# Two fused transformer layers in fp32: a Silu moved behind the feed-forward's copies, and a step of other matmuls put in front of three groups of transposes

## The chip, the cores and the metric

The kernel runs on one core of a Trainium2 chip. The core's engines are TensorE (PE in the profile, its weight loads PEld), VectorE (DVE), ScalarE (ACT), GpSimd (POOL), and SyncE (SP), which issues the transfers (DMA). Each engine takes its instructions in the order in which the program gives them, and waits at the first whose inputs are not there. The metric is the device time of one execution in microseconds (us), given as the median of several runs; lower is better.

## The reference, cut to what matters

Two layers over 1024 positions of width 1024, all in float32. The first mixes a gated delta rule (4 heads, chunks of 64 in the reference) with stick-breaking attention; the second has two kinds of attention, a feed-forward net with a causal convolution, and a small gate at the end. The change touches the delta rule, the projections in front of it, and the feed-forward net:

```python
# first layer
proj = jnp.einsum('bsd,dp->bsp', xn, w_in)
qkv_a = jax.nn.silu(_causal_dwconv(proj[..., :A_QKV1], conv_w)).astype(f32)
q_a = _l2n(qkv_a[..., :nqk].reshape(b, s, DN_HEADS, DN_DK))
...
decay = jnp.exp(jnp.where(causal, gc[..., :, None] - gc[..., None, :], -jnp.inf))
kk = jnp.einsum('bhnid,bhnjd->bhnij', k, k)
m = jnp.where(strict, beta[..., :, None] * kk * decay, 0.0)
sol = lax.linalg.triangular_solve(eye + m, rhs, left_side=True, lower=True, unit_diagonal=True)
...
# second layer
def conv_ffn(h, w_gate, w_up, conv_w, conv_b, w_down):
    s = h.shape[1]
    g = h @ w_gate
    gp = jnp.pad(g, ((0, 0), (CONV_WIDTH - 1, 0), (0, 0)))
    conv = conv_b
    for j in range(CONV_WIDTH):
        conv = conv + gp[:, j:j + s, :] * conv_w[j]
    return (jax.nn.silu(conv) * (h @ w_up)) @ w_down
```

## The kernel before, in words

**Products.** A float32 product is made as three passes of matmuls: every operand is split into a high part (a rounded cast, on ACT) and a low part (what is left, a subtraction on POOL), and high by high, high by low and low by high are summed in PSUM (lines L260 to L262, and L1531 in the feed-forward). A framework orders each engine's instructions by priorities before the program is built; what that order is, the lists in the section on the change show.

**Projections in front of the delta rule (`proj_a`).** Twelve tiles of 128 channels. For each, `conv` does the causal convolution on VectorE (L510, then three times L512) and a Silu on ScalarE (L514, output `conv_s`); `post` then transposes the tile on TensorE (L526, four at a time), and VectorE scales the result into `conv_kv` (L535), which is stored to DRAM (L536). `post` of a tile is issued one projection later than its `conv`; the last two, tiles 10 and 11, have no projection behind them any more.

**The fill.** `fill` is a list of 84 steps of independent work for the other half of the layer (`proj_b`: a projection through `qk_stack`, 48 matmuls of 128x256 a step at its start, then a normalisation: squares on ACT, L738 and L739 on VectorE, a reciprocal root by twelve small VectorE operations `rs_...` of L287 to L302, and a multiplication on POOL, L746). `mix` interleaves it with a main generator: at each `yield` of that one, steps of the fill are issued until both stand at the same share.

**The delta rule (`gdr`).** Eight chunks of 128 positions in two lanes, even and odd, each chunk in 19 steps with a `yield` between them; the second lane begins nine rounds later. Of a chunk: POOL makes `G` (L591), a matmul sums it (L593), ScalarE takes exponentials; products of keys (L608); VectorE makes `NT`; then, in one step, POOL scales `qk` (L616), VectorE makes `XT` from `NT` in two operations (L618, L619), TensorE transposes it (L622), and ScalarE copies the result. A blocked inversion follows (L633, L640).

**The feed-forward (`ffn`).** Eleven rounds (`gi`) of 256 channels. Each has two products, gate and up, each by a Strassen-Winograd scheme (`wino`) of seven half-size products; one of these (`mul`) is 12 matmuls of 128x512. Order of the muls in a product: B11, B21, T2, T1, T3, T4, B22. B11, T2 and T3 add up in one PSUM tile, `x`; between them `keep` copies the sum so far to SBUF (`u1`, `u2`, `u3`, all L1535 on ACT), and the next mul into `x` waits for that copy. `out(ct, half, ...)` hands a finished quarter to VectorE: of the gate product L1567 into `f_u`, of the up product L1582 and L1583. When the gate product is done, VectorE does the convolution over `f_u` for both channel tiles `ct` (L1573 once and L1575 twice for each) and ScalarE a Silu of each (L1576). ScalarE also does the casts of the weights, one mul's at a time and seven muls ahead (L1511), and POOL the low parts (L1512) and the sums of weights (L1517).

Of the kernel before, what the change touches and what calls it, by code (L numbers as in the profile page):

```python
# [15 lines left out]
AF = mybir.ActivationFunctionType  # L16
# [147 lines left out]
class Kern:  # L164
# [22 lines left out]
    def PT(self, shape=(128, 4, 128)):  # L187

        return self.pt.tile(list(shape), F32, tag="pj" if self.pt is self.pj else "pt", name="pt")
# [193 lines left out]
    def layer1(self):  # L383
        nc, d, tc, vec = self.nc, self.d, self.tc, self.vec
        dr = lambda n, s: self.dram.tile(s, F32, name=n)
        self.dr_x = dr("dr_x", [T, D])
        self.dr_v = dr("dr_v", [2, NT, 128, 256])
        self.dr_gate = dr("dr_gate", [128, 16, 1024])
        self.dr_z = dr("dr_z", [2, 128, 4, 1024])
        self.dr_qk = dr("dr_qk", [4, 128, 4, 1024])  # L390
        self.dr_oa = dr("dr_oa", [2, 128, 4, 1024])
        self.dr_qa = dr("dr_qa", [128, 8, 1024])
        self.dr_kv = dr("dr_kv", [128, 2, 4, NT, 128])
        with self.pool("xn1") as xnp:
            self.xn = [self.pair(xnp, f"xn1_{h}") for h in range(2)]
            zp, zp_close = self.open("zp", 2)
            fill = Fill(chain(self.proj_b(), self.proj_z(zp)), 84)
            with self.pool("gdr0") as self.gp:
                with self.pool("cv", 2, "right") as self.cv, self.banks(4, 4):
                    with self.pool("nrm1", 1, "right") as np_:  # L400
                        get = self.loader(d["x"], np_, nc.sync)
                        get(0)
                        g1 = self.gain(np_, "g_n1")
                        get(1)
                        self.wahead = 0
                        wv = self.W(d["w_vba"])
                        get(2)
                        get(3)
                        w = self.W(d["w_qa"][0])
                        self.wahead = 400  # L410
                        get(4)
                        for f in self.later:
                            f()
                        self.norm_half(get, g1, self.xn[0], np_, 0)
                        self.norm_half(get, g1, self.xn[1], np_, 1)
                    self.proj_a(wv, w)
                with self.pool("pb", 1, "right") as self.pb, self.banks(2, 0):
                    self.mix(self.gdr(), fill, 0.43)
            b = self.banks(2, 1)
            self.mix(self.sb(), fill, 0.9)  # L420
            b.close()
            self.pjs = self.banks(5, 3)
            self.mix(self.merge_in(), fill)
            zp_close()
# [65 lines left out]
        self.nb2 = gp.tile([128, 32], F32, name="nb2")  # L490
        nc.vector.tensor_scalar(self.nb2, self.b2, -1.0, None, ALU.mult)

    def proj_a(self, wv, w):
        nc, d, gp, cv = self.nc, self.d, self.gp, self.cv
        ba = gp.tile([128, NT, 8], F32, name="ba")

# [60 lines left out]
        for c in range(2, 12):  # L557
# [5 lines left out]
            post(*pend.pop(0))  # L563
            pend.append((c, conv(c, u)))
        for p in pend:
            post(*p)

    def gdr(self):
# [13 lines left out]
        def chunk(c):  # L582
# [34 lines left out]
            XT = tl("XT")  # L617
            nc.vector.tensor_tensor(XT, NTt, bc(self.m2t), ALU.mult)  # L618
            nc.vector.tensor_tensor(XT, XT, bc(self.ident), ALU.add)  # L619
            px = PT()  # L620
            for h in range(4):
                nc.tensor.transpose(px[:, h, :], XT[:, h, :], self.ident)  # L622
# [87 lines left out]
        n, done = 0, 0  # L710
        while lanes[0] or lanes[1]:
            for p in range(2):
                if p == 1 and n < 9:
                    continue
                if lanes[p]:
                    if next(lanes[p][0], 1) == 1:
                        lanes[p].pop(0)
                        if lanes[p]:
                            next(lanes[p][0])
                    done += 1  # L720
                    yield min(1.0, done / 150)
            n += 1
        es.close()

# [769 lines left out]
        np_close()  # L1494
        m1_close()

    def wino(self, src, pool, out, ahead=400):


        nc = self.nc  # L1500
# [32 lines left out]
        def keep(ps, n):  # L1533
            v = pool.tile([128, 512], F32, tag=f"w_{n}", name=f"w_{n}", bufs=2)
            nc.scalar.copy(v, ps)  # L1535
            return v
        x, z, y = self.PJ(), self.PJ(), self.PJ()
        mul(x, w1, "B11")
        u1 = keep(x, "u1")
        mul(z, w2, "B21")  # L1540
        out(0, 0, z, u1)
        mul(x, w6, "T2", False)
        u2 = keep(x, "u2")
        mul(y, w5, "T1")
        mul(x, w7, "T3", False)
        u3 = keep(x, "u3")
# [7 lines left out]
    def ffn(self):  # L1554

        nc, d, tc, vec = self.nc, self.d, self.tc, self.vec
        with self.pool("ffn", 1) as fp:
            for gi in range(11):
                us, ys = [], []
                for _ in range(2):  # L1560
                    u = fp.tile([128, 2 + T], F32, tag="f_u", name="f_u", bufs=2)
                    nc.vector.memset(u[:, 0:2], 0.0)
# [4 lines left out]
                    nc.vector.tensor_tensor(u, ps, v, ALU.add)  # L1567
                self.wino(d["w_fg"][gi], fp, gate)
                cw = vec["cw2"]
                for ct in range(2):  # L1570
                    c, u = 2 * gi + ct, us[ct]
                    y = fp.tile([128, T], F32, tag="f_y", name="f_y", bufs=2)
                    nc.vector.tensor_scalar(y, u[:, 0:T], cw[:, c, 0:1], vec["cb2"][:, c:c + 1], ALU.mult, ALU.add)  # L1573
                    for j in range(1, 3):
                        nc.vector.scalar_tensor_tensor(y, u[:, j:j + T], cw[:, c, j:j + 1], y, ALU.mult, ALU.add)  # L1575
                    nc.scalar.activation(y, y, AF.Silu)  # L1576
                    ys.append(y)

                def up(ct, half, ps, v):
                    y = ys[ct][:, half * 512:half * 512 + 512]  # L1580
                    c = fp.tile([128, 512], F32, tag="f_c", name="f_c", bufs=1)
                    nc.vector.tensor_tensor(c, ps, v, ALU.add)  # L1582
                    nc.vector.tensor_tensor(y, y, c, ALU.mult)  # L1583
                self.wino(d["w_fu"][gi], fp, up, 400 if gi else 100)
                for ct in range(2):
                    nc.sync.dma_start(self.dr_h[2 * gi + ct], ys[ct])
        self.xb_close()
# [93 lines left out]
```

## Time and profile before

| What | us |
|---|---|
| runs of the kernel before | 2677.5, 2668.34, 2666.72 |
| median of them | 2668.34 |
| the profiled execution, its own time | 2666.2 |
| its span in the profile | 2664.3 |
| TensorE busy in it | 2486.0 (93%) |
| VectorE, GpSimd, ScalarE busy | 1467.1, 1060.1, 856.4 |

The profiled execution took 2666.2 us; the span from the first to the last instruction is 1.9 us less. Sums of the trace are made against that execution, whose time lies 2.1 us under the median of the runs. The mean TensorE clock granted was 0.98 of full speed. TensorE is the engine that is busy nearly always, so that time is to be had almost only where it waits; the busy times of the others say little by themselves.

### The profile page before, as it was taken

To read this page: it belongs to the slowest core of one execution; us is meant where nothing else is said; L and a number is where in the kernel's file an instruction comes from. 1 tells how busy PE (TensorE), PEld (TensorE's weight loads), DVE (VectorE), ACT (ScalarE), POOL (GpSimd) and SP (SyncE) were. 2 spreads that over 40 slices of the span, in tenths; PEclk is the share of its full clock that TensorE was granted. 3 is DMA by queue.
4 is the path that set the end of the run, shared out by engine and by line. 5 is a ranking of instruction groups with operands and counts; after the bars stand their busy time and mean duration, and the time that the engine had idled before them with its cause. 6 is when DMAs were issued, how large, how long until landed. Compare 5 with 4: busy or idle time off the path is not lost.

```text
span 2664.3 us, 38694 instructions
## 1 busy us (share of the span) xinstructions
PE 2486.0 (93%) x15170; PEld 2114.7 (79%) x15170; DVE 1467.1 (55%) x2837; ACT 856.4 (32%) x1559; POOL 1060.1 (40%) x922
## 2 busy tenths in 40 slices
PE   6998999999999999999889969899999999999999
PEld 6888888976777778989777748888777777777789
DVE  6565555366666554457844537657445435534372
ACT  3322222254444342122324425554333333200030
POOL 2524322121222244544533222322787777533322
PEclk9999999999999999999999989999999999999999
DMA  4423222253422355322674356562222222523222
GB/s 162 145 103 109 82 84 77 67 154 103 124 83 72 134 191 183 106 85 80 200 218 140 111 168 180 165 208 88 63 82 77 80 79 68 201 79 111 72 84 92
DMA packets 153006, 313.54 MB, mean 118 GB/s; under 512 B 14164, under 2 KB 57428, under 8 KB 152696
## 3 DMA queue, kind: packets, MB, share of 16 engines
q1 hardware_dynamic: 152824, 311.07, 37.5%
q8 instruction: 120, 1.97, 0.3%
q14 instruction: 62, 0.51, 0.1%
HBM read 214.01 MB, written 100.42 MB: 118 GB/s over the span
## 4 chain that ended last, share of the span: by engine, by line
PE 54%; DVE 13%; DMA 5%; ACT 4%; issue 4%; POOL 1%; SPq 0%; ACTq 0%; DVEq 0%; POOLq 0%
PE pj L1531 15%; PE pj L262 9%; PE pj L261 9%; PE pj L260 9%; PE po L916 3%; PE pt L912 2%; DVE cs L876 2%; DVE e L873 1%; DMA m_o<-dr_oa 1%; PE po L1339 1%; DVE aT L914 1%; DVE cs L877 1%; DMA dr_dqk<-qb_st 1%; DMA dr_mla<-l_st 1%; DVE rs_a L300 1%
## 5 line engine op out<-in xcount | busy, mean ns | idle before, releaser
L251 POOL TENSOR_SCALAR hl<-raw 128x512 fp32r<-128x512 f32 (+3 forms) x270 | 196.4, 733 | 932.7 <-PE pj L262 920.0
L252 POOL TENSOR_TENSOR hl<-raw,hl 128x512 fp32r<-128x512 f32 (+3 forms) x270 | 372.3, 1385 | 16.1
L260 PE MATMUL pj<-hl,xn_0h 128*128 128x256 f32 (+2 forms) x544 | 161.2, 297 | 2.0 <-DVE qb_st L310 1.2
L261 PE MATMUL pj<-hl,xn_0h 128*128 128x256 f32 (+2 forms) x544 | 160.9, 296 | 1.7 <-POOL hl L252 1.7
L262 PE MATMUL pj<-hl,xn_0l 128*128 128x256 f32 (+2 forms) x544 | 160.0, 294 | 0.0
L260 PE MATMUL pj<-hl,xn_1h 128*128 128x256 f32 (+2 forms) x544 | 158.4, 291 | 0.0
L262 PE MATMUL pj<-hl,xn_1l 128*128 128x256 f32 (+2 forms) x544 | 158.0, 290 | 0.0
L261 PE MATMUL pj<-hl,xn_1h 128*128 128x256 f32 (+2 forms) x544 | 157.5, 289 | 0.0
L1512 POOL TENSOR_TENSOR hl<-w_s,hl 128x512 fp32r<-128x512 f32 x88 | 121.8, 1384 | 83.2 <-ACT hl L1511 82.9
L262 PE MATMUL pj<-hl,f_hl 128*128 128x512 f32 x352 | 140.5, 401 | 2.8 <-DVE f_hl L1613 2.7
L260 PE MATMUL pj<-hl,f_hh 128*128 128x512 f32 x352 | 140.0, 398 | 2.6 <-DVE xres L1622 2.1
L261 PE MATMUL pj<-hl,f_hh 128*128 128x512 f32 x352 | 138.2, 393 | 0.0
L914 DVE COPY aT<-pt 128x512 f32<-128x512 f32 (+1 forms) x128 | 80.5, 629 | 102.6 <-PE pt L912 101.7
L1622 DVE TENSOR_TENSOR xres<-xres,pj 128x512 f32<-128x512 f32 x96 | 65.2, 686 | 126.4 <-PE pj L262 114.6
L1512 POOL TENSOR_TENSOR hl<-raw,hl 128x512 fp32r<-128x512 f32 x66 | 99.2, 1508 | 71.4 <-ACT hl L1511 70.8
L1567 DVE TENSOR_TENSOR f_u<-pj,w_u 128x512 f32<-128x512 f32 x44 | 30.5, 692 | 170.3 <-ACT w_u L1535 96.4
L916 PE MATMUL po<-aT,v 128*64 128x128 f32 x1152 | 98.2, 287 | 26.1 <-DVE aT L914 21.1
L916 PEld LDWEIGHTS po<-aT,v 128*64 128x64 f32 x1152 | 59.8, 136 | 73.2 <-DVE aT L914 53.3
L260 PE MATMUL pj<-xn_0h,hl 128*128 128x512 f32 x288 | 116.9, 406 | 0.0
L260 PE MATMUL pj<-xn_1h,hl 128*128 128x512 f32 x288 | 115.8, 402 | 0.0
L262 PE MATMUL pj<-xn_1h,hl 128*128 128x512 f32 x288 | 115.5, 401 | 0.0
L262 PE MATMUL pj<-xn_0h,hl 128*128 128x512 f32 x288 | 115.1, 400 | 0.0
(594 smaller groups left out, 7392.9 us busy)
## 6 DMA issues: line engine op xcount, KB each, us to landing
raw<-in_w_o_dram SPq DMA_DIRECT2D x28, 512.0 KB
qk<-dr_mla SPq DMA_DIRECT2D x32, 416.0 KB
dr_mla<-l_st SPq DMA_DIRECT2D x32, 384.0 KB
raw<-in_w_fg_dram SPq DMA_DIRECT2D x22, 512.0 KB
raw<-in_w_fu_dram SPq DMA_DIRECT2D x22, 512.0 KB
dr_h<-f_y SPq DMA_DIRECT2D x22, 512.0 KB
raw<-in_w_fd_dram SPq DMA_DIRECT2D x22, 512.0 KB
f_y<-dr_h SPq DMA_DIRECT2D x22, 512.0 KB
```

The lines of the kernel that those rows point to most:

```text
L251: nc.gpsimd.tensor_scalar(hl[:, 0], raw[:, k:k + c], 1.0, 1.0, ALU.mult, ALU.mult)
L252: nc.gpsimd.tensor_tensor(hl[:, 1], raw[:, k:k + c], hl[:, 0].bitcast(F32), ALU.subtract)
L260: mm(ps, lh[0], rh[0], start=first, stop=False)
L261: mm(ps, lh[0], rh[1], start=False, stop=False)
L262: mm(ps, lh[1], rh[0], start=False, stop=last)
L876: nc.vector.tensor_tensor_scan(cs[:, a, ::-1], self.ones[:, 0:1].to_broadcast([128, nk]), e[:, a, ::-1], 0.0, ALU.mult, ALU.add)
L912: nc.tensor.transpose(pt[:, b, :], e[a][:, j * 128:j * 128 + 128], self.ident)
L914: copy[j0 > 0](aT[:, :n], pt[:, :n])
L916: nc.tensor.matmul(po[64 * a:64 * a + 64, :], v[:, j, a * 64:a * 64 + 64], aT[:, b, :], start=j == 0, stop=j == i)
L1512: nc.gpsimd.tensor_tensor(hl[:, 1], v, hl[:, 0].bitcast(F32), ALU.subtract)
L1531: nc.tensor.matmul(ps, w[k][l], b[r][:, k, :], start=first and k + n == 0, stop=k == 3 and n == 2, skip_group_check=not first)
L1622: nc.vector.tensor_tensor(xr, xr, ps, ALU.add)
```

## The change

Three parts. **(1)** `proj_a` takes `fill`, and does one step of it in front of each of the last two `post`; the pool `pb`, from which these steps draw their tiles, is opened earlier for that, on the other side of SBUF. **(2)** `chunk` has one more `yield`, between `XT` and its transposes, the second lane begins one round later, and the share is counted over 158 instead of 150. **(3)** `keep` can be given something to do behind a copy. In `ffn` the Silu of channel tile 1 is now issued behind the copy `u1` of the up product, that of tile 0 behind the copy `u2`; the convolutions are written for tile 1 first; and quarter (0, 0) of each product is handed out behind `u2`'s copy instead of in front of the mul T2.

```diff
-                    self.proj_a(wv, w)
-                with self.pool("pb", 1, "right") as self.pb, self.banks(2, 0):
+                    self.pb, pb_close = self.open("pb")
+                    self.proj_a(wv, w, fill)
+                with self.banks(2, 0):
                     self.mix(self.gdr(), fill, 0.43)
+                pb_close()
...
         for p in pend:
+            fill.step()
             post(*p)
...
             nc.vector.tensor_tensor(XT, XT, bc(self.ident), ALU.add)
+            yield
             px = PT()
...
-                if p == 1 and n < 9:
+                if p == 1 and n < 10:
...
-                    yield min(1.0, done / 150)
+                    yield min(1.0, done / 158)
...
             nc.scalar.copy(v, ps)
+            if n in then:
+                then[n]()
             return v
...
-        out(0, 0, z, u1)
         mul(x, w6, "T2", False)
         u2 = keep(x, "u2")
+        out(0, 0, z, u1)
...
-                for ct in range(2):
+                ys = {}
+                for ct in (1, 0):
...
-                    nc.scalar.activation(y, y, AF.Silu)
-                    ys.append(y)
+                    ys[ct] = y
+                silu = lambda y: nc.scalar.activation(y, y, AF.Silu)
...
-                self.wino(d["w_fu"][gi], fp, up, 400 if gi else 100)
+                self.wino(d["w_fu"][gi], fp, up, 400 if gi else 100,
+                          {"u1": lambda: silu(ys[1]), "u2": lambda: silu(ys[0])})
```

The lines of the changed kernel stand 3 (delta rule), 4 (`qk_stack` and the later steps of the delta rule) or 5 to 8 (feed-forward) below those of the kernel before: L591 becomes L594, L622 becomes L626, L746 becomes L750, L1535 becomes L1540, L1576 becomes L1585.

**In the feed-forward**, ScalarE's queue around an up product stands so before (L1511 casts weights, L1535 are the copies of `keep`, L1576 the Silu; here 18619 is the convolved tile 0 and 18624 tile 1):

```order
L1511 CAST hl_18778<-raw_18774 128x512
L1511 CAST hl_18781<-raw_18776 128x512
L1535 COPY w_u1_18677<-pj_18662 128x512
L1511 CAST hl_18788<-w_s_18786 128x512
L1576 ACTIVATE f_y_18619<-f_y_18619 128x1024
L1576 ACTIVATE f_y_18624<-f_y_18624 128x1024
L1511 CAST hl_18791<-w_s_18784 128x512
L1535 COPY w_u2_18706<-pj_18662 128x512
```

and so in the changed kernel (18619 is now tile 1, 18623 tile 0):

```order
L1516 CAST hl_18778<-raw_18774 128x512
L1585 ACTIVATE f_y_18619<-f_y_18619 128x1024
L1516 CAST hl_18781<-raw_18776 128x512
L1540 COPY w_u1_18675<-pj_18660 128x512
L1585 ACTIVATE f_y_18623<-f_y_18623 128x1024
L1516 CAST hl_18788<-w_s_18786 128x512
L1516 CAST hl_18791<-w_s_18784 128x512
L1540 COPY w_u2_18702<-pj_18660 128x512
```

The two Silu operations have parted, and the first of them stands in front of a cast and of the copy `u1`, the second between that copy and `u2`: the scheduler has put each ahead of where it is written.

VectorE's queue at the same place, from the last quarters of the gate product (L1567) over the convolution (L1573, L1575) to the first quarter of the up product (L1582), before:

```order
L1567 TENSOR_TENSOR f_u_18772<-pj_18878,w_u3_18875 128x512
L1567 TENSOR_TENSOR f_u_18770<-pj_18809,w_u2_18849 128x512
L1573 TENSOR_SCALAR f_y_18905<-f_u_18770,cw2_75,cb2_76 128x1024
L1573 TENSOR_SCALAR f_y_18910<-f_u_18772,cw2_75,cb2_76 128x1024
L1575 SCALAR_TENSOR_TENSOR f_y_18905<-f_u_18770,cw2_75,f_y_18905 128x1024
L1575 SCALAR_TENSOR_TENSOR f_y_18910<-f_u_18772,cw2_75,f_y_18910 128x1024
```

and in the changed kernel:

```order
L1574 TENSOR_TENSOR f_u_18772<-pj_18878,w_u3_18875 128x512
L1581 TENSOR_SCALAR f_y_18905<-f_u_18772,cw2_75,cb2_76 128x1024
L1583 SCALAR_TENSOR_TENSOR f_y_18905<-f_u_18772,cw2_75,f_y_18905 128x1024
L1574 TENSOR_TENSOR f_u_18770<-pj_18809,w_u2_18848 128x512
L1583 SCALAR_TENSOR_TENSOR f_y_18905<-f_u_18772,cw2_75,f_y_18905 128x1024
L1581 TENSOR_SCALAR f_y_18909<-f_u_18770,cw2_75,cb2_76 128x1024
L1569 MEMSET f_u_19056 128x2
L1583 SCALAR_TENSOR_TENSOR f_y_18909<-f_u_18770,cw2_75,f_y_18909 128x1024 x2
```

The convolution of tile 1 (`f_u_18772`) now begins one quarter of the gate product earlier and is done as a whole ahead of that of tile 0; before, both began behind the last quarter and took turns.

**In front of the delta rule**, GpSimd's queue, from the low parts of a weight (L252) to the first chunk's second operation, before:

```order
L252 TENSOR_TENSOR hl_2400<-raw_2395,hl_2400 128x512
L591 TENSOR_TENSOR G_1843<-cst_85,g_a_826 128x512
L616 TENSOR_TENSOR qk_1839<-qk_1839,EG_1847 128x1024
L591 TENSOR_TENSOR G_2144<-cst_85,g_a_826 128x512
L746 TENSOR_TENSOR qb_raw_1871<-qb_raw_1871,rs_y_2064 128x1024
```

and in the changed kernel:

```order
L252 TENSOR_TENSOR hl_2321<-raw_2316,hl_2321 128x512
L750 TENSOR_TENSOR qb_raw_1806<-qb_raw_1806,rs_y_1982 128x1024
L594 TENSOR_TENSOR G_1967<-cst_85,g_a_829 128x512
L619 TENSOR_TENSOR qk_1963<-qk_1963,EG_1971 128x1024
L594 TENSOR_TENSOR G_2223<-cst_85,g_a_829 128x512
```

The fill's multiplication, which waits for the reciprocal root of that step on VectorE, has moved from behind the first two `G` to in front of them.

**In the delta rule**, TensorE's queue between a chunk's products of keys and its transposes, in a chunk in the middle, before (rows of the fill, L260 to L262, left out at the line of dots):

```order
L608 MATMUL inv<-qk 128x256 x4
L633 MATMUL inv<-X,NT 128x64 x4
L262 MATMUL pj<-hl,xn_0l 128x256
...
L622 MATMUL inv<-cst,XT 128x128 x4
L640 MATMUL inv<-Y,XT 128x64 x4
```

and in the changed kernel:

```order
L611 MATMUL inv<-qk 128x256 x4
L637 MATMUL inv<-X,NT 128x64 x4
...
L644 MATMUL inv<-Y,XT 128x64 x4
L262 MATMUL pj<-hl,xn_0l 128x256
...
L648 MATMUL inv<-cst,X 128x128 x4
L261 MATMUL pj<-hl,xn_0h 128x256
L626 MATMUL inv<-cst,XT 128x128 x4
L654 MATMUL inv<-X,NT 64x64 x4
```

The transposes of `XT` now stand behind one step of the other lane (L644, L648), with fill around it.

## Rows read from the trace of the kernel before

**Rows 1.** Windows: us, busy PE, PEld, DVE, ACT, POOL (instructions); clock, DMA share, GB/s.
```profile
215.00:220.00 5.00, 5.00 (x32) 5.00 (x33) 2.67 (x4) 1.74 (x2) 0.00 (x0) 0.71 0.38 124
...
230.00:520.00 290.00, 273.43 (x2225) 258.07 (x2225) 151.96 (x414) 74.94 (x150) 84.77 (x68) 0.99 0.24 75
```

**Rows 2.** Waits of TensorE, whole span: total us, times, longest.
```profile
PE pj L1531 <- ACT w_u L1535: 13.6, 11, 1.5
...
PE inv L622 <- DVE XT L619: 9.2, 7, 1.9
...
PE pt L526 <- ACT conv_s L514: 4.9, 2, 4.7
```

**Rows 3.** Timeline of TensorE in one round: T2, T1, T3 of the up product.
```profile
1923.62 0.40 PE L1531 MATMUL pj<-T2h,hl 128*128 128x512 f32 x1
...
1926.40 0.40 PE L1531 MATMUL pj<-T1h,hl 128*128 128x512 f32 x1
...
1930.60 0.50 PE L1531 MATMUL pj<-T3h,hl 128*128 128x512 f32 x1 [1.25 <-ACT w_u L1535]
```

**Rows 4.** Timeline of ScalarE in the same round.
```profile
1921.09 0.62 ACT L1511 CAST hl<-raw 128x512 fp32r<-128x512 f32 x1 [2.17 <-PE pj L1531]
1921.62 0.58 ACT L1535 COPY w_u<-pj 128x512 f32<-128x512 f32 x1
...
1927.30 2.26 ACT L1576 ACTIVATE f_y<-f_y 128x1024 f32<-128x1024 f32 x2 [2.77 <-DVE f_y L1575]
```

**Rows 5.** Timeline of VectorE in the same round, cut into single instructions.
```profile
1915.49 0.69 DVE L1567 TENSOR_TENSOR f_u<-pj,w_u 128x512 f32<-128x512 f32 x1 [0.89 <-PE pj L1531]
...
1918.99 1.86 DVE L1573 TENSOR_SCALAR f_y<-f_u,cw,cb 128x1024 f32<-128x1024 f32 x1
...
1920.78 0.80 DVE L1573 TENSOR_SCALAR f_y<-f_u,cw,cb 128x1024 f32<-128x1024 f32 x1
1921.50 1.27 DVE L1575 SCALAR_TENSOR_TENSOR f_y<-f_u,cw,f_y 128x1024 f32<-128x1024 f32 x1
```

**Rows 6.** Timeline of GpSimd in the same round.
```profile
1916.26 1.29 POOL L1512 TENSOR_TENSOR hl<-w_s,hl 128x512 fp32r<-128x512 f32 x1 [0.40 <-ACT hl L1511]
...
1919.00 1.30 POOL L1512 TENSOR_TENSOR hl<-raw,hl 128x512 fp32r<-128x512 f32 x1
```

**Rows 7.** Timelines elsewhere: VectorE, then GpSimd, at two close starts.
```profile
1646.61 1.90 DVE L1324 SCALAR_TENSOR_TENSOR e<-e,a_r 128x512 f32<-128x512 f32 x1
...
2302.04 1.23 DVE L1613 TENSOR_TENSOR f_hl<-f_y,f_hh 128x1024 fp32r<-128x1024 f32 x1 [0.45 <-ACT f_hh L1612]
...
1646.65 1.31 POOL L252 TENSOR_TENSOR hl<-raw,hl 128x512 fp32r<-128x512 f32 x1
...
2302.16 2.27 POOL L252 TENSOR_TENSOR hl<-raw,hl 128x512 fp32r<-128x512 f32 x1
```

**Rows 8.** Timelines in front of the delta rule: VectorE, ScalarE, GpSimd.
```profile
211.79 0.69 DVE L535 TENSOR_TENSOR conv_kv<-pt,srk 128x512 f32<-128x512 f32 x1 [3.59 <-DMA dr_kv<-conv_kv]
212.40 1.28 DVE L512 SCALAR_TENSOR_TENSOR conv_y<-conv_u,cw,conv_y 128x1024 f32<-128x1024 f32 x1
...
225.19 0.17 DVE L297 TENSOR_SCALAR rs_i<-rs_m 128x16 int32<-128x16 int32 x1
...
213.79 1.06 ACT L514 ACTIVATE conv_s<-conv_y 128x1024 f32<-128x1024 f32 x1 [11.44 <-DVE conv_y L512]
...
232.35 1.90 POOL L746 TENSOR_TENSOR qb_raw<-qb_raw,rs_y 128x1024 f32<-128x1024 f32 x1 [2.05 <-DVE rs_y L302]
```

**Rows 9.** Timelines at a chunk's `XT`: VectorE, GpSimd, TensorE.
```profile
402.81 1.78 DVE L618 TENSOR_TENSOR XT<-NT,cst 128x512 f32<-128x512 f32 x1
404.62 1.41 DVE L619 TENSOR_TENSOR XT<-XT,cst 128x512 f32<-128x512 f32 x1
...
401.65 2.39 POOL L616 TENSOR_TENSOR qk<-qk,EG 128x1024 f32<-128x1024 f32 x1 [3.02 <-ACT XT L645]
...
406.18 0.63 PE L622 MATMUL inv<-cst,XT 128*128 128x128 f32 x4 [1.17 <-DVE XT L619]
```

More of the change, by code (lines that the diff above doesn't have):

```diff
@@ L491, in kstats, with proj_a @@
         nc.vector.tensor_scalar(self.nb2, self.b2, -1.0, None, ALU.mult)
-    def proj_a(self, wv, w):
+    def proj_a(self, wv, w, fill):
         nc, d, gp, cv = self.nc, self.d, self.gp, self.cv
@@ L1495, in out2b, with wino @@
         m1_close()
-    def wino(self, src, pool, out, ahead=400):
+    def wino(self, src, pool, out, ahead=400, then={}):
         nc = self.nc
@@ L1558, in ffn @@
             for gi in range(11):
-                us, ys = [], []
+                us = []
                 for _ in range(2):
```

## The prediction

> **What bounds the kernel now.** I read the waits of TensorE first, because that engine is busy 93% of the span: a change can only give time where it stands still, or take time by making it stand. Three of its waits belong to what is changed [rows 2]: the mul T3 waits for a copy in each of the eleven rounds of the feed-forward, 13.6 us in all; the transposes of `XT` wait seven times, 9.2 us; and the last transposes of `proj_a` wait once for 4.7 us. Then I read timelines around one case of each. In the windows the stretch of the delta rule has TensorE busy for 273.43 of 290 us [rows 1]: much more than these waits is not there.
>
> **The feed-forward before.** In the round shown T2 starts at 1923.62 and T1 at 1926.40, so a mul takes 2.78 us and T3 could start at 1929.18. It starts at 1930.60 [rows 3], 1.42 late, and 11 times that is 15.6 us (the waits view models where a matmul ends and gives 13.6). It waits for the copy `u2`, which stands behind both Silu operations, begun at 1927.30 [rows 4], and these wait for the end of the convolution. The convolution is slow because VectorE and GpSimd shut each other out. A TENSOR_SCALAR takes 0.80 alone, but 1.86 when it starts at 1918.99 beside GpSimd's operation at 1919.00; it ends 0.55 behind that one's end at 1920.30 [rows 5, 6]. The other way round, GpSimd's operation of 2302.16 lasts 2.27 instead of 1.3 and ends 1.16 behind VectorE's of 2302.04 to 2303.27 [rows 7]. Each waits for the whole of the other.
>
> **The feed-forward after.** Nothing is added or removed; two Silu operations and half of a convolution move. The convolution of tile 1 can start when L1567 of its last quarter is done, at 1915.49 + 0.69 = 1916.18, some 1916.22 with the 0.04 that lie between two such operations. GpSimd's low part starts at 1916.26 [rows 5, 6]. Which of the two goes first is the question on which this part hangs, since VectorE would be ahead by only about 0.04. In the round of before VectorE was ahead by 0.01 and lost; at 1646.61 it was ahead by 0.04 and lost (1.90 us for 512 columns, and it ended 0.55 behind GpSimd's); at 2302.04 it was ahead by 0.12 and won [rows 5, 6, 7]. The nearest case is a loss, and I take it.
>
> Then: low part to 1917.55; TENSOR_SCALAR to 1918.10; GpSimd's next operation, already waiting, to 1919.26 (+1.16); the first L1575 to 1920.35 (its own time is 1.27 [rows 5]; behind a wait I take 1.1, since part of it is done by then); GpSimd to 1921.5; the second L1575 to 1922.6. The Silu of tile 1 takes 1.06 for that size [rows 8] (1.13 by the pair in [rows 4]), to 1923.7. Behind it in ScalarE's order stand a cast and then `u1`, which are 0.53 apart, and the copy takes 0.58 [rows 4], overlapping a little: done at 1924.7. T2 needs that copy. It started at 1923.62 and will start at about 1924.77: **a new stall of 1.15**, because the first Silu stands in front of `u1`. What is queued behind the Silu is the cast, whose low part is wanted only seven muls later, so that alone costs nothing. The convolution of tile 0 follows: TENSOR_SCALAR to 1923.4, L1575 to 1924.7, one GpSimd operation to 1925.9, L1575 to 1927.0, Silu to 1928.1, two casts, `u2` done near 1929.7. T3 can then start at 1924.77 + 2 x 2.78 = 1930.33, so its own stall is gone, with 0.6 to spare. Saved: 15.6 - 11 x 1.15 = **3.0 us**. The bounds of the term: 15.6 if no stall is left, and below, nothing (a T2 stall as long as the T3 stall was). Handing out (0, 0) behind `u2` moves L1582 of VectorE, for which no matmul waits before the mul B22, eight us later.
>
> The Trainium skill, page "SBUF — State Buffer", section "SBUF: two separate sides", says that VectorE and GpSimd share a port pair as an exclusive lock, and that whichever starts first holds it for its whole instruction. That both shut each other out whole agrees with 1.86 and 2.27; that the first to start wins does not agree with 1918.99 and 1646.61, where the later one by record won. By its rule VectorE would win at 1916.22; that is the first rival below.
>
> **The front.** Before, TensorE has nothing left at 210 and waits 4.7 us for the Silu of tile 11 [rows 2], which ends at 213.79 + 1.06. That Silu waited for L512 of 212.40, and this stood in VectorE's queue behind L535, which waited 3.59 for the store that held its buffer [rows 8]. Then the clock falls: 0.71 was granted from 215 to 220, which is 0.29 x 5 = 1.45 us more. In the changed order all three L512 of tile 11 come ahead of the waiting L535, so the Silu is ready near 210.2. A further 39 matmuls of the fill stand in front of the last transposes: each of the two steps has 48, of which the scheduler had 57 there already. At 273.43 / 2225 = 0.123 us each [rows 1] they take 4.8 us, and fill the gap; as they are taken from later, TensorE's work is the same. Gain: 4.7 + 1.45 = 6.15.
>
> But `G` of the first chunk now stands on GpSimd behind the fill's multiplication L746, and the first matmul of the delta rule needs `G`. From the end of the last transposes: four VectorE operations of 0.69 (two L535, L738, L739), 2.8; twelve small ones of 0.17 and a gap between [rows 8], 2.5; L746, 1.90 [rows 8]; `G`, as 1.3 like other GpSimd operations of 512 columns [rows 6]. Together 8.5, against 4.8 of matmuls that stand in front: a **new wait of 3.7**. TensorE standing that long, I count the clock's 1.45 again. Before, `G` was made long ahead and none of this was there. Net: 6.15 - 5.15 = **1.0 us**. Bounds: +6.15 if the chain is hidden, and -3.8 if none of those matmuls covers it (8.5 + 1.45 - 6.15).
>
> **The delta rule.** The wait at the transposes is one for VectorE: `XT` takes 1.78 and 1.41, since L618 and L619 both lie beside GpSimd's L616, which shuts them out from 401.65 on, and its follower [rows 9]. From the end of L608 near 401.3 to 406.18 this takes 4.9 us. I summed TensorE's work between the two in both orders: 2.9 to 4.4 us before, and 3.9, 4.1, 4.3, 4.3, 5.0, 5.2, 5.6, 7.9 for the eight chunks after, since a step of the other lane and its fill now lie between. Against the 4.9 that leaves 0.9 + 0.8 + 0.6 + 0.6 = 2.9 of waits; of 9.2 some **6.3 us** are saved, bounds 0 (the wait goes on to L633 or L640, the next to need `X`) and 9.2. The lanes keep their pace otherwise: the same fill is spread over 158 shares instead of 150, less the 39 matmuls.
>
> **The sum.** 3.0 + 1.0 + 6.3 = 10.3 us off the profiled execution's 2666.2: **2656 us**. The median of the runs shown is 2668.34, 2.1 above that execution; 2656 is 0.46% under the median. A difference of 0.5%, 13.3 us, is about what a measurement of this kernel can tell from no change: faster means below 2655.0, slower above 2681.7.
>
> **Rivals.**
> *VectorE wins at 1916.22.* Then TENSOR_SCALAR ends at 1917.02, GpSimd at 1918.2, L1575 at 1919.3, GpSimd at 1920.4, L1575 at 1921.5, the Silu at 1922.6, `u1` at 1923.6: T2 stalls 0.04 and T3, by the same steps, 0.14. Saved 15.6 - 2.0 = 13.6 instead of 3.0: 2666.2 - 13.6 - 7.3 = 2645.3. For it: VectorE is ahead, and wins at 0.12; against it: two losses at 0.01 and 0.04. It decides at a lead somewhere between 0.04 and 0.12. The rule of the Trainium skill named above gives this outcome.
> *The delta rule gives nothing.* The chain from `NT` over `XT` and `X` to L633 and L640 is as long as before, and if the other lane's step needs the same VectorE, the wait only goes on to the next matmul. For it: VectorE's 1.78 and 1.41 do not shrink. Against: 2.9 of 9.2 is what the order leaves. 2666.2 - 3.0 - 1.0 = 2662.2, up to 2666 if the front gives nothing too.
> *Slower: the added step lengthens the chain.* Each lane has eight steps more. A step is 290 / 150 = 1.93 us long; if the lanes and not TensorE set the pace, the stretch grows by 8 x 1.93 = 15.5 us. 2666.2 + 15.5 - 3.0 - 1.0 = 2677.7. It ends slower than before once more than 4.0 of these 15.5 us are not covered. For it: at `XT` the lane does set the pace. Against: TensorE is busy 94% of the stretch [rows 1], and the fill is handed out by shares, so it does not run out earlier.
>
> **Chances.** The forecast (GpSimd wins, the front and the delta rule as summed) 0.48, its own range 2649 to 2662; VectorE wins 0.18, 2643 to 2653 by what the delta rule gives; the delta rule gives nothing 0.27; slower than before 0.07. The range that leaves out 2 in 10 goes from 2643 to 2666. Of the forecast a little under half lies below 2655.0, with the first rival 0.41 faster; of the last rival's share about 0.05 lies above 2681.7, since more than one step may be exposed; the rest, 0.54, is within 0.5%.
>
> **What would show it.** In the waits of TensorE after: L1531 for `u2` gone, and a wait of T2 for `u1` of about 1.1, eleven times; if that is 0.1 or less, VectorE won. The TENSOR_SCALAR of tile 1 at 1.8 to 1.9 us says GpSimd won, 0.8 that it lost. The 4.7 us of L526 gone, and a wait of 3 to 4 us at L596 (before L593) for GpSimd's `G`, with a clock near 0.7 behind it. L626 (before L622) waiting for some 3 us instead of 9.2. The prediction is wrong if a wait appears at L637 or L644 as large as the one that goes, if the stretch of the delta rule grows, or if the convolution of tile 0 loses a further turn and `u2` is late as well: each such turn is 1.1 x 11 = 12 us.

## The result, and the profile after

| | us |
|---|---|
| the changed kernel, median of 4 runs | 2649.93 (2642.67 to 2655.23) |
| the kernel before, beside it, 4 runs | 2670.65 (2666.72 to 2677.5) |
| ratio | 0.9915, 95% interval 0.9896 to 0.9933 |
| the changed kernel once more, 5 runs, and before, 14 runs | 2648.8 and 2673.58; ratio 0.9906, 0.989 to 0.9922 |
| span of the profiled execution, before and after | 2664.3 and 2647.3 |

The change makes the kernel faster by 0.9%, which is twice what was forecast: 2656 us had been said, 10.3 us under the profiled execution of before. Between the two traces lie 17.0 us, between the medians 20.7 and 24.8. The execution profiled before was one of the quicker ones of its kernel, so a sum made against it understates what the medians show.

These are the waits of TensorE in the changed kernel over its whole span (total us, times, longest), those that answer to [rows 2] and two new ones:

```profile
PE pj L1536 <- ACT w_u L1540: 10.6, 10, 2.0
...
PE inv L596 <- POOL G L594: 3.0, 1, 3.0
...
PE inv L626 <- DVE XT L622: 1.7, 3, 0.8
...
PE pj L1536 <- DVE f_c L1590: 1.4, 1, 1.4
```

The wait of 13.6 us for `w_u` has become one of 10.6, and a wait for `f_c` has come. The wait for `XT` has gone from 9.2 to 1.7 us. The 4.7 us in front of the last transposes are gone, and 3.0 us for `G` stand there instead. The windows of both kernels show how much time TensorE gained where the delta rule and what stands ahead of it are computed. Columns as in [rows 1]; first the kernel before, a row that answers for the whole stretch:

```profile
190.00:520.00 330.00, 307.82 (x2445) 289.12 (x2443) 174.52 (x445) 82.62 (x163) 99.52 (x78) 0.98 0.26 82
```

and the changed kernel, with three windows of 5 us out of it:

```profile
190.00:520.00 330.00, 319.44 (x2539) 299.78 (x2538) 168.57 (x469) 84.68 (x167) 101.05 (x81) 0.99 0.28 86
215.00:220.00 5.00, 5.00 (x46) 5.00 (x45) 3.35 (x7) 1.88 (x2) 0.00 (x0) 1.00 0.28 105
225.00:230.00 5.00, 4.54 (x24) 3.74 (x25) 0.60 (x1) 2.23 (x6) 0.40 (x1) 1.00 1.03 252
440.00:445.00 5.00, 4.66 (x32) 4.46 (x32) 2.11 (x4) 1.17 (x2) 1.90 (x1) 0.71 0.74 262
```

In 330 us TensorE stands still for 10.6 instead of 22.2 us. The low clock of 215 to 220 is not there, and none came behind the wait for `G`, which ends at 225.5; one is left at 440. So 11.6 of the 17.0 us between the traces are standing time in this stretch.

The round of the feed-forward that answers to [rows 3 to 6], in the changed kernel: TensorE, ScalarE, VectorE and GpSimd.

```profile
1909.96 0.50 PE L1536 MATMUL pj<-T2h,hl 128*128 128x512 f32 x1 [0.95 <-ACT w_u L1540]
...
1907.86 1.07 ACT L1585 ACTIVATE f_y<-f_y 128x1024 f32<-128x1024 f32 x1 [3.71 <-DVE f_y L1583]
1908.83 0.60 ACT L1516 CAST hl<-raw 128x512 fp32r<-128x512 f32 x1
1909.33 0.58 ACT L1540 COPY w_u<-pj 128x512 f32<-128x512 f32 x1
...
1900.71 0.69 DVE L1574 TENSOR_TENSOR f_u<-pj,w_u 128x512 f32<-128x512 f32 x1 [0.89 <-PE pj L1536]
1901.43 1.89 DVE L1581 TENSOR_SCALAR f_y<-f_u,cw,cb 128x1024 f32<-128x1024 f32 x1
1903.36 2.20 DVE L1583 SCALAR_TENSOR_TENSOR f_y<-f_u,cw,f_y 128x1024 f32<-128x1024 f32 x1
...
1901.48 1.29 POOL L1517 TENSOR_TENSOR hl<-w_s,hl 128x512 fp32r<-128x512 f32 x1 [0.40 <-ACT hl L1516]
```

TENSOR_SCALAR starts by record at 1901.43, 0.05 ahead of GpSimd's start, and takes 1.89 (0.80 alone, [rows 5]): GpSimd won, as in the forecast. The Silu then ends at 1908.93, the cast and the copy follow, and T2 starts at 1909.96 behind a wait. T2 waits in ten of the eleven rounds, T3 in none.

### The profile page after: what moved, and what is told of

Same layout as the page of the kernel before. It is cut to its first block, busy times and chain, and to the rows that moved or that the text cites. A ratio compares the mean times of both kernels' runs of the same rounds, so it can differ in the third digit from the quotient of the medians.

```text
span 2647.3 us, 38679 instructions
## 1 busy us (share of the span) xinstructions
PE 2480.8 (94%) x15170; PEld 2111.9 (80%) x15170; DVE 1450.7 (55%) x2837; ACT 855.3 (32%) x1559; POOL 1061.1 (40%) x922
## 4 chain that ended last, share of the span: by engine, by line
PE 50%; DVE 15%; DMA 5%; ACT 4%; issue 4%; POOL 2%; SPq 0%; ACTq 0%; DVEq 0%; POOLq 0%
PE pj L1536 12%; PE pj L262 9%; PE pj L260 9%; PE pj L261 9%; PE po L920 3%; PE pt L916 2%; DVE cs L880 2%; DVE f_y L1583 1%; DVE e L877 1%; DMA m_o<-dr_oa 1%; PE po L1343 1%; DMA f_y<-dr_h 1%; DVE aT L918 1%; DVE cs L881 1%; POOL hl L252 1%
## 5 line engine op out<-in xcount | busy, mean ns | idle before, releaser
L252 POOL TENSOR_TENSOR hl<-raw,hl 128x512 fp32r<-128x512 f32 (+3 forms) x270 | 368.6, 1371 | 16.3
L260 PE MATMUL pj<-hl,xn_0h 128*128 128x256 f32 (+2 forms) x544 | 161.3, 297 | 1.7 <-DVE qb_raw L742 1.1
L262 PE MATMUL pj<-hl,xn_0l 128*128 128x256 f32 (+2 forms) x544 | 160.7, 295 | 0.0
L260 PE MATMUL pj<-hl,xn_1h 128*128 128x256 f32 (+2 forms) x544 | 158.2, 291 | 0.0
L262 PE MATMUL pj<-hl,xn_1l 128*128 128x256 f32 (+2 forms) x544 | 157.0, 289 | 0.0
L262 PE MATMUL pj<-hl,f_hl 128*128 128x512 f32 x352 | 139.8, 399 | 3.7 <-DVE f_hl L1622 3.7
L260 PE MATMUL pj<-hl,f_hh 128*128 128x512 f32 x352 | 139.3, 396 | 3.7 <-POOL hl L252 1.9
L260 PE MATMUL pj<-xn_0h,hl 128*128 128x512 f32 x288 | 117.2, 407 | 0.0
L260 PE MATMUL pj<-xn_1h,hl 128*128 128x512 f32 x288 | 115.8, 402 | 0.0
L262 PE MATMUL pj<-xn_1h,hl 128*128 128x512 f32 x288 | 115.4, 401 | 0.0
L262 PE MATMUL pj<-xn_0h,hl 128*128 128x512 f32 x288 | 115.2, 400 | 0.0
L261 PE MATMUL pj<-xn_0l,hl 128*128 128x512 f32 x288 | 114.6, 398 | 0.0
```

Source lines behind the costliest of these rows:

```text
L252: nc.gpsimd.tensor_tensor(hl[:, 1], raw[:, k:k + c], hl[:, 0].bitcast(F32), ALU.subtract)
L260: mm(ps, lh[0], rh[0], start=first, stop=False)
L261: mm(ps, lh[0], rh[1], start=False, stop=False)
L262: mm(ps, lh[1], rh[0], start=False, stop=last)
```

## The experiments

All ratios are to the kernel before, run beside the others on the same chip. The runs were made in three groups, in which its medians were 2674.39 (the three parts and the pinned order), 2673.58 (the changed kernel once more, the steps behind, the early `G`, the lead) and 2670.25 (one step, three steps, the best). The us given behind a ratio are what its distance from 1 makes of that median.

**The three parts alone.** Each of the three first kernels has one part of the diff and nothing else. The feed-forward:

```diff
+            if n in then:
+                then[n]()
...
+                self.wino(d["w_fu"][gi], fp, up, 400 if gi else 100,
+                          {"u1": lambda: silu(ys[1]), "u2": lambda: silu(ys[0])})
```

> The feed-forward part of the change alone (the Silu operations, the order of the convolutions, quarter (0, 0) later). My theory, by the trace of the changed kernel: the wait of T3 is exchanged for one of T2 that is nearly as long, so this part is worth 1 to 3 us: 0.999 of the time before, T2 late by about 1.1 us in nine rounds, T3 in none. The rival, that the feed-forward gave more than the trace shows because the whole kernel gained 20 us in the median: 0.997 or less.

Measured: 2669.94, ratio 0.9987 (0.9971 to 1.0003). The waits of the feed-forward are those of the changed kernel, and from its first matmul to its last it takes 445.60 us, as in the changed kernel (445.67; before 447.28). Its trace has a use beyond that: from 190 to 520 it is the kernel before, in another execution.

```profile
190.00:520.00 330.00, 308.31 (x2404) 289.82 (x2403) 174.29 (x445) 81.18 (x160) 94.09 (x73) 0.96 0.26 82
210.00:220.00 10.00, 5.42 (x31) 5.22 (x30) 4.55 (x6) 2.94 (x3) 0.00 (x0) 0.66 0.51 187
230.00:240.00 10.00, 8.08 (x44) 7.71 (x43) 4.60 (x14) 1.19 (x2) 3.51 (x3) 0.68 0.19 54
390.00:400.00 10.00, 6.97 (x37) 6.62 (x36) 8.42 (x25) 1.66 (x3) 2.98 (x2) 0.70 0.87 255
```

TensorE is busy as long as before (308.31 against 307.82), but has done 41 matmuls fewer in it, some 7 of them because it came to this stretch 0.9 us later. The three windows of 10 us hold waits of 4.6, 1.9 and 3.0 us and a fall of the clock to the lower of its two levels (1.2 instead of 2.4 GHz); their means are 0.66, 0.68 and 0.70. In the trace of before the same windows have the same waits and 0.83 each: the clock fell there too, for a shorter time.

The yield:

```diff
             nc.vector.tensor_tensor(XT, XT, bc(self.ident), ALU.add)
+            yield
             px = PT()
...
```

> The added step of the delta rule alone (the yield between XT and its transposes, the second lane a round later, 158 shares). Theory 1: the added step hides the wait at the transposes of XT and nothing else: 8 to 9 us, 0.9968, the wait of TensorE for XT falls from 9.2 to about 2 us, and the 4.7 us in front stay. Theory 2: the step also moves the fill against the chunks' other steps, and with that the waits behind the normalisation's transposes (3.0 us for a reciprocal root, 1.2 us more) go too: 11 to 14 us, 0.995. If it is under 3 us, the gain came from the fill's two steps.

Measured: 2667.55, ratio 0.9979 (0.9963 to 0.9994), 5.6 us. The waits of TensorE from 190 to 520 (total us, times, longest):

```profile
PE pt L526 <- ACT conv_s L514: 4.9, 1, 4.9
PE inv L641 <- DVE o_m L697: 3.5, 2, 3.0
PE inv L623 <- DVE XT L619: 3.2, 2, 1.9
```

The wait for `XT` fell from 9.2 to 3.2, nearly as summed. The wait of 3.0 at the inversion stays at the same matmul, now put down to another operation of VectorE, so theory 2 is not what the yield does. Theory 1 is right for the wait and too high for the time: its 8 to 9 us lie at the far end of the interval (1.6 to 9.9), and TensorE's standing time from 190 to 520 falls only from 22.2 to 18.6, since waits of 0.6 to 1.6 us came at other places.

The two steps of the fill:

```diff
         for p in pend:
+            fill.step()
             post(*p)
```

> The two steps of the fill in front of the last transposes alone. Theory: the wait of 4.7 us and the low clock behind it go (6.2 us), a wait of 3 us for the first G comes: 3 us net, 0.9988, and the waits at XT stay at 9 us. Rival: taking 39 matmuls of cover away from the delta rule costs as much there as it gives in front: no difference.

Measured: 2657.79, ratio 0.9944 (0.9927 to 0.996), 15 us. Both expectations failed: by its median this is the largest part of the change, and it had been given 1.0 us in the prediction.

```profile
PE inv L625 <- DVE XT L622: 7.1, 8, 1.2
PE inv L596 <- POOL G L594: 2.9, 1, 2.9
...
PE inv L643 <- DVE rs_a L300: 0.9, 2, 0.6
```

The front is as forecast, a wait of 2.9 for one of 4.7, with a granted clock of 0.74 behind it (225 to 230). The wait for `XT` is shorter too, although nothing was put in front of it, and the 3.0 us at the inversion are gone.

**Where the 15 us come from.** The same two steps, but behind both of the last transposes:

```diff
         for p in pend:
             post(*p)
+        for _ in range(2):
+            fill.step()
```

> The kernel before with the pool opened earlier and the two steps of the fill issued at the same point, but behind both of the last transposes instead of one in front of each: the fill is as far ahead as in the run of that part alone, the gap for the Silu stays (4.7 us), and G does not stand behind the fill's multiplication. Theory 1: most of the 15 us of that part come from where the advance puts the fill's later steps against the chunks (the 3.0 us wait at the inversion goes, and with it a fall of the clock): 8 to 13 us, 0.996. Theory 2: they come from the cover of the gap: within 3 us of before.

Measured: 2664.98, ratio 0.9974 (0.9962 to 0.9986), 7 us (4 to 10). The gap is there, so these 7 us have nothing to do with its cover: theory 1's mechanism, a little under its range.

```profile
PE inv L626 <- DVE XT L623: 7.3, 8, 1.2
PE pt L528 <- ACT conv_s L516: 4.6, 1, 4.6
...
PE inv L644 <- DVE rs_a L300: 0.9, 2, 0.6
```

Behind the front the waits are those of the run with the steps in front: the 3.0 us are gone here too. It is the fill's advance that does this, not its place in front of the transposes. Then one step, and three:

```diff
-        for p in pend:
-            post(*p)
+        post(*pend[0])
+        fill.step()
+        post(*pend[1])
```

> The kernel before with one step of the fill, not two, in front of the last transposes (behind those of tile 10). Theory 1: what the two steps gave beyond the gap is a matter of where the fill's normalisations meet the chunks' steps, so one step gives something else: the 3.0 us wait at the inversion may stay or return elsewhere, and the gain lies anywhere between 2 and 15 us without being half of 15. Theory 2: the advance acts by its length as cover: half of it, 7 us, 0.9973, with half of the change in the waits.

Measured: 2676.77, ratio 1.0017 (1.0001 to 1.0033): no gain, if anything a loss, where both theories had a gain of 2 us or more. The waits of TensorE from 190 to 540, and below them the first of two new ones on TensorE, VectorE and GpSimd:

```profile
PE pt L528 <- ACT conv_s L516: 5.7, 1, 5.7
PE pj L260 <- DVE qb_st L310: 4.8, 1, 4.8
PE st L705 <- POOL ot L701: 3.9, 3, 3.4
...
261.09 0.55 PE L260 MATMUL pj<-hl,xn_0h 128*128 128x256 f32 x1 [4.81 <-DVE qb_st L310]
...
255.44 2.29 DVE L302 SCALAR_TENSOR_TENSOR rs_y<-rs_a,rs_y 128x16 f32<-128x16 f32 x1
...
255.35 2.34 POOL L619 TENSOR_TENSOR qk<-qk,EG 128x1024 f32<-128x1024 f32 x1 [0.19 <-issue]
```

An operation of the fill's normalisation, 0.17 alone, takes 2.29 because GpSimd's scaling of `qk` had started 0.09 earlier, and what TensorE needs next (`qb_st`) stands behind it on VectorE. That is 2.1 of the 4.8 us; the rest was not followed further. Three steps:

```diff
         for p in pend:
+            fill.step()
             post(*p)
+        fill.step()
```

> The kernel before with three steps of the fill, the third behind the last transposes. G still stands behind the fill's first multiplication on GpSimd, but 87 matmuls (10.3 us) now stand in front of its matmul instead of 39 (4.6 us), so its wait of 2.9 us goes, as the chain behind the last transposes takes 7.5 us. Theory 1: the waits in the delta rule come out otherwise again, since the normalisations meet other steps: anything from 8 to 19 us. Theory 2 (the longer the advance the better): 18 us or more, 0.993.

Measured: 2660.62, ratio 0.9955 (0.994 to 0.997), 12 us. The wait for `G` is 1.9 and not gone; the wait for `XT` is 5.7. None, one, two and three steps thus give 0, -5, 15 and 12 us. Two and three are not told apart by their intervals, but one step does not give half of two: the gain does not follow the length of the advance, which is what theory 1 said.

**The same stretch in all these runs.** From the first transposes of `proj_a` to the last matmul into `st`, with which the delta rule ends, TensorE has the same number of matmuls to do in every run, 3020 by the traces. A window over exactly this stretch gives its length, and, less busy PE, TensorE's standing time. In this order: before; before, in the trace of the feed-forward part; the yield; two steps in front; two behind; one; three; the changed kernel.

```profile
82.64:534.50 451.86, 428.79 (x3019) 388.63 (x3020) 244.38 (x550) 115.45 (x216) 140.73 (x117) 0.99 0.30 95
83.50:539.92 456.42, 433.83 (x3020) 393.58 (x3020) 244.49 (x550) 115.35 (x216) 140.57 (x117) 0.97 0.30 94
82.81:533.01 450.20, 430.74 (x3020) 391.70 (x3021) 241.03 (x550) 115.51 (x216) 141.03 (x117) 0.98 0.30 96
83.95:527.76 443.81, 427.43 (x3019) 386.51 (x3020) 238.21 (x550) 115.29 (x216) 139.06 (x117) 0.99 0.31 97
82.18:526.91 444.73, 426.11 (x3019) 385.64 (x3020) 236.82 (x550) 115.16 (x216) 140.22 (x117) 1.00 0.30 97
83.10:540.58 457.48, 431.91 (x3019) 392.43 (x3020) 242.11 (x550) 114.97 (x216) 139.38 (x117) 0.97 0.29 94
82.95:523.70 440.75, 426.65 (x3020) 387.59 (x3021) 239.73 (x550) 115.27 (x216) 138.81 (x117) 0.99 0.30 98
83.37:518.70 435.33, 424.77 (x3020) 386.38 (x3020) 232.16 (x550) 115.47 (x216) 139.15 (x117) 0.99 0.31 99
```

With the two steps in front the stretch is 8 us shorter than in the trace of before and 13 shorter than in the other execution of the same code; with the two steps behind it is 0.9 us longer than with them in front. So in these traces the fill's advance gives nearly all that the part gives here, and the cover of the gap about 1 us. They are one execution each, and the first two rows show 4.6 us between executions of one order.

**The new wait for G.** `G` of the first chunk is made ahead of the fill's steps:

```diff
+        self.G0 = gp.tile([128, 4, 128], F32, name="G0")
+        nc.gpsimd.tensor_tensor(self.G0, self.triu[:, None].to_broadcast([128, 4, 128]), self.g[:, 0, :, None].to_broadcast([128, 4, 128]), ALU.mult)
         for p in pend:
             fill.step()
...
-            G = tl("G", own=False)
+            G = self.G0 if c == 0 else tl("G", own=False)
...
```

> The changed kernel with the first chunk's G made in front of the two steps of the fill, so that it does not stand behind the fill's multiplication on GpSimd. Theory: the wait of 3.0 us for G goes and nothing takes its place for long: 2 to 4 us less than the changed kernel. Rival: the next operations of the chunk are late in the same way (VectorE is still busy with the reciprocal root), so the wait moves to the products of keys or to XT, and the time stays.

Measured: 2648.86 (2642.3 to 2651.82), the median of the changed kernel. Its trace has no wait for `G` and none that took its place. By the median the rival is right. But three us are as much as these intervals leave open, and in the stretch just shown the wait's length does come back: it takes 432.45 us with the early `G` (435.33 and 434.84 in the two traces of the changed kernel), and 432.07 in the run of the best below (434.80 in the pinned one without `G`).

**The feed-forward's two questions.** The lead: the cast of one weight in two halves, so that GpSimd starts later.

```diff
-                nc.scalar.copy(hl[:, 0], v)
+                for q in range(parts):
+                    n = slice(q * 512 // parts, (q + 1) * 512 // parts)
+                    nc.scalar.copy(hl[:, 0, n], v[:, n])
...
-            w3 = split(add(a12, s2, ALU.subtract))
+            w3 = split(add(a12, s2, ALU.subtract), 2)
```

> The changed kernel with the cast of one weight, that of the product B22, cut into two halves of 256 columns on ScalarE, so that GpSimd's low part of it starts some 0.1 us later; the computation is the same. Theory: VectorE lost the start of tile 1's convolution because it was only 0.05 us ahead; with 0.15 or more it wins, TENSOR_SCALAR of tile 1 takes 0.8 instead of 1.9 us, T2's wait falls from 1.1 to 0.0 to 0.2 us a round, and the time falls by 8 to 11 us against the changed kernel. Rival: GpSimd wins whatever the lead, and nothing changes.

Measured: 2636.23, ratio 0.987 (0.9849 to 0.9892). The medians lie 12.6 us under the changed kernel, the ratios 9.6; the feed-forward takes 437.63 us from its first matmul to its last instead of 445.68, so 8.0 us less in the trace. VectorE, then GpSimd, in a round:

```profile
1900.51 0.81 DVE L1583 TENSOR_SCALAR f_y<-f_u,cw,cb 128x1024 f32<-128x1024 f32 x1
...
1900.65 1.82 POOL L1519 TENSOR_TENSOR hl<-w_s,hl 128x512 fp32r<-128x512 f32 x1 [0.52 <-ACT hl L1518]
```

With a lead of 0.14 VectorE wins, and GpSimd waits. A tenth of a microsecond on ScalarE decided some 1 us in nearly every round. This is the first rival's case, brought about on purpose. But the lead by record is not all: the trace of before has a place where VectorE is ahead by as little as at 1646.61 [rows 7], 0.04, and wins, since it takes 1.27 and GpSimd 2.40:

```profile
204.67 1.27 DVE L512 SCALAR_TENSOR_TENSOR conv_y<-conv_u,cw,conv_y 128x1024 f32<-128x1024 f32 x1
...
204.71 2.40 POOL L252 TENSOR_TENSOR hl<-raw,hl 128x512 fp32r<-128x512 f32 x1
```

There VectorE went on from another operation of its own without a gap. Whether that is what decides was not tested, and at 1085.12, ahead by 0.03 and without a gap too, it lost (1.73 us where 1.27 is usual).

The order: both Silu operations pinned behind the copies.

```diff
-                silu = lambda y: nc.scalar.activation(y, y, AF.Silu)
+                silu = lambda y: tc.keep_in_program_order(nc.scalar.activation(y, y, AF.Silu))
```

> The changed kernel with both Silu operations pinned behind the copies on ScalarE (behind u1 and behind u2), where the source writes them and the scheduler had not put them. Theory: T2's wait of 1.1 us is the price of the Silu in front of u1, so it goes in all rounds and T3's does not come back: 11 to 14 us less than the changed kernel, 0.987 of the time before. Rival: the Silu only moves the wait on, to T3 or to the quarters handed out later, and the time is that of the changed kernel.

Measured: 2637.43, ratio 0.9867 (0.9846 to 0.9888), as the theory had it. The feed-forward takes 432.33 us, 13.3 less than in the changed kernel. Of the waits of its two products one is left, and ScalarE's row shows the copy in its natural place, ahead of the Silu:

```profile
PE pj L1536 <- DVE f_c L1590: 1.4, 1, 1.4
...
1900.99 0.58 ACT L1540 COPY w_u<-pj 128x512 f32<-128x512 f32 x1
1902.01 1.06 ACT L1585 ACTIVATE f_y<-f_y 128x1024 f32<-128x1024 f32 x1 [0.43 <-DVE f_y L1583]
```

**The best of it.** The changed kernel with the pinned Silu operations and the early `G` (the two diffs above together).

> The changed kernel with both Silu operations pinned behind their copies and the first chunk's G made in front of the fill's steps. Theory: T2 and T3 both without a wait (13 us less than the changed kernel) and no wait for G (3 us, of which the run with G alone showed nothing in the median): 0.986 of the time before; 0.985 if the wait for G is worth its length.

Measured: 2635.39, ratio 0.9864 (0.9836 to 0.9891): faster than both kernels, and the same as the pinned one without the early `G`.

The changed kernel, unaltered, was run again for comparison with all of these:

> The changed kernel once more, unaltered, beside the others on one chip: 0.9915 of the time before, as first measured. The three parts alone gave 0.9987, 0.9979 and 0.9944; if they add up, 0.991.

Measured: 0.9906 (0.989 to 0.9922); the product of the three parts, 0.9987 x 0.9979 x 0.9944, is 0.991. As far as the intervals tell, the parts add up. In the stretch of the delta rule the standing time falls by 3.6 (the yield) and 6.7 us (the two steps) alone and by 12.5 together, a little more than the sum.

## Why the prediction came out as it did

**The feed-forward: right in mechanism, and nearly in size.** Forecast were a new stall of T2 of 1.15 a round, none of T3, and 3.0 us saved. In the round shown B21's first matmul starts at 1906.07, so T2 could start at 1908.85; it starts at 1909.96, 1.11 late. The waits went from 13.6 to 10.6 + 1.4 = 12.0, so 1.6 us in the trace, and the whole feed-forward from 447.28 to 445.67. The half that was missed: the first round waits 2.0, and the last round has a wait of B22 for `f_c` of 1.4 that was not there before; that `f_c` stands on VectorE behind two operations of the next product (L1622), and no run shows whether the later quarter (0, 0) brought it about. The measurement of the part alone, by its interval between a loss of 1 and a gain of 8 us, holds both numbers. The choice on which the term hangs, that GpSimd wins, came out in all eleven rounds, with a lead of 0.05 lost, and the other outcome came with a lead of 0.14. The choice was weaker than it was put: it names losses at 0.01 and 0.04 as the nearest cases and passes over the win at 204.67, with the same lead of 0.04. The rule of the Trainium skill, page "SBUF — State Buffer", section "SBUF: two separate sides", that the first to start holds the ports, agrees with the leads of 0.12 and 0.14 and with 204.67, and not with 1646.61 and 1901.43.

**The delta rule's added step: right for the wait.** Forecast were 6.3 us, with 2.9 of waits left for `XT` (4.9 - 3.9 is 1.0, not 0.9, a difference of 0.1). With the yield alone the wait for `XT` fell to 3.2, with the fill's steps beside it to 1.7. The part alone measured 5.6 us (0.9979, interval 2 to 10); its standing time fell by 3.6, as other waits grew, so that the two sizes lie so close is in part luck.

**The front: the step that was mis-sized.** The term was 1.0 us, and the part measured 15 (0.9944, interval 11 to 20). What the prediction described did happen, and nearly as it was worked out: the gap went, a wait for `G` came, of 3.0 instead of 3.7, and the clock fell behind it in the part alone, though not in the changed kernel. The cover of the gap is worth about what the term said: 0.9 us between the steps in front and the steps behind, in the rows of the stretch. What failed is the sentence that the 39 matmuls "are taken from later", with nothing else said of later, and in the part on the delta rule that "the lanes keep their pace otherwise". An advance of the fill by two steps moves each of its normalisations against the chunks' steps, and these meet on VectorE and GpSimd. Shown: the same advance without the cover of the gap gives 7 us, by the ratio and by the stretch (451.86 to 444.73), and one step gives none, with two new waits of 4.8 and 3.4. For the first 4.8 the trace has the meeting itself, for the other places it is an inference from waits that came and went. I had no row that says how such a meeting will come out, but the bounds could have been wider: the waits at the inversion and the normalisations, in the trace of before 3.0 us at one place, belonged to the price of moving the fill.

**What is left between 7 and 15.** The traces say where most of it does not come from. Between the last matmul into `st` and the feed-forward TensorE does the same 8040 matmuls in the same order in every run here, and no edit touches them. They take 1320.25 us in the trace with the steps in front and 1324.77 in that with the steps behind, which is 4.5 of the 5.8 us between the spans of these two; over the thirteen traces they take from 1318.77 to 1330.02, with a granted clock of 0.97 in the shortest and 0.96 in the longest. A part of the 15 us goes with the granted clock of the executions. The mean of it was 0.977 over 23 runs of before, 0.981 over 6 runs with the two steps in front and 0.980 over 9 with the steps behind; in the runs of before, which are one program, a span of 2664.0 us goes with 0.98 and one of 2679.7 with 0.973. Taken only at 0.979 to 0.981, six runs of before have a mean of 2667.8 us and the six with the steps in front one of 2659.0: 9 us, not 15. That fewer and shorter waits let the clock fall less often, so that the rest belongs to the change as well, fits this and was not tested by itself.

**The rivals.** VectorE winning at the close start did not come (but was produced, with 8.0 us in the feed-forward's own stretch and 12.6 between medians, against 10.6 worked out). The delta rule did not give nothing, and the added step did not lengthen the chain: its waits shrank, and no wait of its size came at L637 or L644 (those at L706 for GpSimd's `ot`, 1.6 us in all, became 2.8).

## What to carry to other kernels

Work that is interleaved by shares is not only cover: moving it by a step moves its later meetings with the main work, and one step more or less can be worth more than the gap that it was moved for, or nothing at all. Try several advances, and read the waits at the meetings, not only at the place that was edited. And read the scheduled order, not the source: here both Silu operations were written behind the copies and stood in front of them, and pinning them gave some four tenths of the whole change once more.

## What the runs showed of the hardware

In the close starts shown here VectorE and GpSimd excluded each other for whole instructions, and a small lead by record does not say who goes first. VectorE lost with a lead of 0.05 us in the changed kernel's round and won with 0.14 in the same place when a cast was cut in two; with 0.04 it lost at 1646.61 and won at 204.67. What decides at such leads stays open.

One program has a spread of 0.6% that goes with TensorE's granted clock: 23 runs of the kernel before lie between 2665.86 and 2682.15 us, the longer ones at the lower clock. The same matmuls with the same waits took 451.86 and 456.42 us in two executions (mean clock 0.99 and 0.97), and 8040 matmuls in one and the same order took 1318.77 to 1330.02 us. One profile of each of two kernels therefore cannot tell a few us over the whole span; stretch by stretch, with standing time and clock beside each other, it can tell more.
